# Modulation rows on 32 partitions with fillers between them, angle steps split around the first moving tile, and two weight sums one product later

## The chip, the cores and the metric

The kernel runs on one core of a Trainium2 chip, in one launch. The metric is the time of that launch on the device, in microseconds. The engines are named as in the profile: PE multiplies matrices, PEld is its weight load, DVE (vector), ACT (scalar) and POOL work element by element, SP issues most transfers, and DMA carries them.

## The reference, cut to what matters

The block works on x (2048 rows of 1024) with a conditioning vector c. What concerns us is its head: the modulated norm that makes the input h of the large product, and the angles for the rotary positions.

```
c_act = silu(c)
ada = (c_act @ w_ada + b_ada)[:, None, :]          # 1024 -> 3072
shift, scale, gate = split(ada, 3)
h = rms(x, g_pre) * (1 + scale) + shift            # 2048 x 1024
proj = h @ w_in                                    # 1024 -> 4864
q, k, v, z_a, u_b, v_b, z_b, g_logits = split(proj)
q, k = rope(q, positions), rope(k, positions)      # cos and sin of position * inv_freq
...
y_a = window_attention(q, k, v, sinks) * silu(z_a)
y_b = chunked_gating(gelu(u_b), gelu(v_b)) * silu(z_b)
merged = sigmoid(g_a) * (y_a @ w_proj_a) + sigmoid(g_b) * (y_b @ w_proj_b)
out = x + gate * rms(merged @ w_out, g_post)
```

## The kernel before, in words

**Products.** Every large product is cut into halves three ways and done in the Strassen-Winograd form: seven half-size products (p = 0 to 6) instead of eight. Each uses a weight tile W (a quadrant of the weights, or a sum or difference of quadrants) and a moving tile T (the same of h). Each tile is kept as a rounded high part and a low rest, and `mm3` (L163) multiplies high by high, high by low and low by high: 12 matmuls of 128x512 per product and block. `w_of` (L214) prepares a W: ACT casts the high part at once, and DVE's subtraction for the low part is put on a list that `low_now` (L177) empties later. `want(n)` (L192) prepares all W tiles up to number n; it empties that list first, so the low part of tile n-1 is issued when tile n is prepared. It also calls the transfers some tiles ahead (`fetch_to`, up to a limit `cap`) and the sums that the tile needs (`sum_to`).

**Sums.** `combos` (L243) lists, for one block's seven products, in front of which product each sum of quadrants is issued: s1 and s3 (A21+A22 and A11-A21), s2, s4. For the first four blocks (`first`) DVE makes them, for later blocks POOL. Sums that are kept go to memory a step later.

**Order.** The order on each engine is the order of the program, written out by hand; each engine works through its own list and waits only for data and for free buffers. `step` (L229) runs one product of one block, with hooks before, in the middle and after it; `later(n, f)` hangs f onto the n-th step from now. Tiles have pools with fixed numbers of buffers.

**The head (L761 to L796).** It runs before the first step. Plain filler matmuls (`warm`, L521, a matrix of ones into a bank that is overwritten later) run on PE at the start. The parts, each named as it is used below:

- `positions` and `rope_do(n)` (L663, L621): DVE turns the positions into reduced angles in 24 steps, each a DVE operation on 128x512; `rope_do(n)` issues the next n. `rope_out` (L613) takes their sine on ACT and stores two tiles.
- `squares`, `square_sums`, `rstd`, `rstd_out` (L630 to L661), for half h of the rows of x (`h` = 0, 1): ACT squares eight tiles, DVE adds them, four small PE matmuls sum over partitions, DVE copies (L652), POOL raises to the power -1/2, PE spreads the result over 128 partitions (L658), ACT copies it out (L661).
- `ada_row(hf, kks)` (L680): the modulation rows for half hf of the features. For each of eight slices kk, two matmuls in float32: c_act's column kk, broadcast to 64 columns, against 512 columns of w_ada. Their results stand on partitions 0 to 63 and 64 to 127 of one bank, 64 equal copies of each row. `ada_rows_out` (L690) copies that bank to SBUF on ACT, and `ada_fin` (L694) turns rows into columns by four small matmuls with a picked identity, after which three or four short DVE operations make the scale A and the shift SH (L704, L707).
- `t_part(p, i)` (L751): step i of six for the moving tile of product p: `scaled` (L675, DVE, x times A times the norm), a difference where the product needs one, the high part on ACT (L739, L741), the low part on DVE (L746, L748).

In the order of the program, the head issues 7 angle steps around the squares of the first half, `rstd(0)`, rows 0 and 1, `rstd_out(0)`, 13 angle steps, rows 2 to 7 without a break, W tiles 0 and 1 with both low parts, the loads of the second half of w_ada, the last 4 angle steps, then `ada_rows_out(0)`, `ada_fin(0)`, the squares of the second half between the parts of the first moving tile, W tiles 2 and 3, the sums of the squares, and `rope_out`.

After that the steps begin: product 0 of blocks 0 to 3 (banks X/Y, s and b); behind the third of them `rstd(1)`, behind the fourth `second_half` (L1307): `rstd_out(1)`, all eight slices of `ada_row(1)` on PE, the DVE sums for product 1, and the moving tile of product 1. Then product 1 of the four blocks, and so on to product 6. From block 4 on each block does its seven products in a row.

Of the kernel before, what the change touches and what calls it, by code (L numbers as in the profile page):

```python
# [15 lines left out]
P = 128  # L16
# [34 lines left out]
NFIRST = 4  # L51
# [4 lines left out]
def hybrid_block(ctx: ExitStack, tc: tile.TileContext, xt, x, wada, wgate, wI, wP, wO,  # L56
                 colc, rowc, bs, sinks, ws, pos, consts, mcp, out):
    nc = tc.nc
    act, dve, pool, pe, sp = nc.scalar, nc.vector, nc.gpsimd, nc.tensor, nc.sync
# [3 lines left out]
    sb = ctx.enter_context(tc.tile_pool(name="sb", bufs=1))  # L63
# [23 lines left out]
    def flat(tag, dt=F32):  # L87
        return t2(tag, [P, 512], dt)

    def const(shape, name, dt=F32):  # L90
        return cp.tile(shape, dt, tag=name, name=name)
# [4 lines left out]
    def bank():  # L96
        return pb.tile([P, 512], F32, tag="b", name=nm("b"))
# [35 lines left out]
    ident, mC = cst[:, 0:P], cst[:, P : 2 * P]  # L133
# [19 lines left out]
    def psub(o, a, b, op=ALU.subtract):  # L153
        pool.tensor_tensor(out=o, in0=a, in1=b, op=op)  # L154
# [17 lines left out]
    loads, preps, sums, ready = [], [], [], []  # L172
# [4 lines left out]
    def low_now():  # L177
        while due:
            due.pop(0)()

    def fetch_to(k):
        while cur["load"] < len(loads) and loads[cur["load"]][0] <= min(k, cur["cap"]):
            loads[cur["load"]][1]()
            cur["load"] += 1

    def sum_to(n):
        while cur["sum"] < min(n, len(sums)):
            for f in sums[cur["sum"]]:
                f()
            cur["sum"] += 1  # L190

    def want(n):  # L192

        while cur["prep"] < min(n + 1, len(preps)):
            k = cur["prep"]
            fetch_to(k + 4)
            low_now()
            sum_to(k + 1)
            ready.append(w_of(preps[k]()))
            sum_to(k + 1 + cur["ahead"])  # L200
            fetch_to(k + 5)
            cur["prep"] += 1
# [11 lines left out]
    def w_of(src):  # L214
        w = w_new()
        act.copy(w[:, 0, :], src)  # L216
        due.append(lambda: sub(w[:, 1, :], src, w[:, 0, :].bitcast(F32)))
        return w
# [3 lines left out]
    def later(n, f, post=False):  # L222
        hooks.setdefault((slot[0] + n, post), []).append(f)
# [19 lines left out]
    def combos(env, n, first):  # L243

        def keep(i, t):
            if n is not None:
                later(1, lambda: sp.dma_start(sS[n][i], t))

        second = sub if first else psub


        two = "A22" if first else "A11"

        def s1():
            env["S1"] = flat("S")
            (add if first else lambda o, a, b: psub(o, a, b, ALU.add))(env["S1"], env["A21"], env["A22"])
            keep(0, env["S1"])

        def s3():
            second(env["A21"], env["A11"], env["A21"])  # L260
            keep(2, env["A21"])

        def s2():
            env["S2"] = env[two]
            second(env["S2"], env["S1"], env["A11"])
            keep(1, env["S2"])

        def s4():
            low_now()
            second(env["A12"], env["A12"], env["S2"])  # L270
            keep(3, env["A12"])

        def last():
            return env["A22b"] if first else env["A22"]

        sums.extend([[], [s1], [s2], [], [s3], [s4], []] if first else [[s1, s3], [], [s2], [], [s4], [], []])
        preps.extend([lambda k=k: env[k] for k in ("A11", "S1", "S2", "A12", "A21", "A12")] + [last])

    def stream_fresh(quads, n=None):
# [232 lines left out]
    cact = const([P, 16], "cact")[:, 0:KT]  # L512
# [8 lines left out]
    def warm(n, m=4):  # L521
        for _ in range(n):
            pe.matmul(BK["X"][:, 0 : m * P], ones, wide[:, 0:m, :], start=True, stop=True, skip_group_check=True)
# [89 lines left out]
    def rope_out():  # L613
        for i, k in ((1, 2), (0, 0)):
            t = ropew[:, k, :]
            act.activation(out=t, in_=t, func=AF.Sin)
            sp.dma_start(cs_s[i], t)
# [3 lines left out]
    def rope_do(n):  # L621
        for _ in range(n):
            next(rope_it, None)
# [6 lines left out]
    def squares(h, kts, now=True):  # L630
        for kt in kts:
            if kt == 0:
                sq[h] = flat("e")
                act.activation(out=sq[h], in_=xh[kt][h], func=AF.Square)
            else:
                t = flat("m") if now or kt < 5 else flat("e")
                act.activation(out=t, in_=xh[kt][h], func=AF.Square)
                sq_of.append(t)
                if now:
                    square_sums(h)  # L640

    def square_sums(h):
        while sq_of:
            add(sq[h], sq[h], sq_of.pop(0))
# [11 lines left out]
    def rstd_out(h, b):  # L656
        for i in range(4):
            pe.matmul(b[:, i * P : (i + 1) * P], rs0[h][:, i : i + 1].broadcast_to([P, P]), ident,  # L658
                      start=True, stop=True, skip_group_check=True)
        rbs[h] = flat("e")  # L660
        act.copy(rbs[h], b)  # L661
# [16 lines left out]
    rows = {}  # L678

    def ada_row(hf, kks):  # L680

        if hf not in rows:
            rows[hf] = rows.get("bank") or bank()
        for kk in kks:
            for i in range(2):
                pe.matmul(rows[hf][64 * i : 64 * (i + 1), :], cact[:, kk : kk + 1].broadcast_to([P, 64]),  # L686
                          adaw[hf][kk // 4][:, kk % 4, i * 512 : (i + 1) * 512],
                          start=kk == 0, stop=kk == KT - 1, skip_group_check=True)

    def ada_rows_out(hf):  # L690
        rows[hf, "sb"] = flat("e")
        act.copy(rows[hf, "sb"], rows[hf])

    def ada_fin(hf):  # L694

        o = rows.get("bank") or bank()
        for kt in range(4):
            pe.matmul(o[:, 2 * kt : 2 * kt + 2], rows[hf, "sb"][:, kt * P : (kt + 1) * P], ident[:, 0:P:64],
                      start=True, stop=True, skip_group_check=True)
        o2 = o[:, 0:8].rearrange("p (n two) -> p two n", two=2)  # L700
        c4 = slice(4 * hf, 4 * hf + 4)

        def tt(dst, a, b, op):
            dve.tensor_tensor(out=dst, in0=a, in1=b, op=op)  # L704

        tt(A[:, c4], o2[:, 1], col[:, C_BSC + 4 * hf : C_BSC + 4 * hf + 4], ALU.add)
        dve.scalar_tensor_tensor(out=A[:, c4], in0=A[:, c4], scalar=1.0, in1=col[:, C_GPRE + 4 * hf : C_GPRE + 4 * hf + 4],  # L707
                                 op0=ALU.add, op1=ALU.mult)
        tt(SH[:, c4], o2[:, 0], col[:, C_BSH + 4 * hf : C_BSH + 4 * hf + 4], ALU.add)
        if hf:  # L710
            tt(DS, SH[:, 4:8], SH[:, 0:4], ALU.subtract)
# [39 lines left out]
    def t_part(p, i):  # L751

        if i < 4:
            t_y(p, i)
        if 1 <= i < 5:
            t_d(p, i - 1)
            t_hi(p, i - 1)
        if i >= 2:
            t_lo(p, i - 2)
# [10 lines left out]
    warm(6)  # L770
    rstd(0, BK["Z"])
    ada_row(0, range(0, 2))
    rstd_out(0, BK["W"])
    rope_do(13)
    ada_row(0, range(2, 8))
    want(1)
    low_now()
    ada_load(1)
    cur["cap"] = 3 * NFIRST - 1
    rope_do(26)  # L780
    ada_rows_out(0)
    warm(1, 2)
    ada_fin(0)
    warm(3)
    squares(1, range(0, 2), False)
    for i in range(6):
        t_part(0, i)
        if i == 2:
            want(2)
        elif i == 4:  # L790
            low_now()
        squares(1, range(i + 2, i + 3), False)
    want(NFIRST - 1)
    square_sums(1)
    low_now()
    rope_out()  # L796


# [457 lines left out]
    def run_all():  # L1256
        nonlocal T

        for s in range(NS):
# [38 lines left out]
            if s == 0:  # L1298
# [8 lines left out]
                def second_half():  # L1307
                    rstd_out(1, BK["W"])
                    ada_row(1, range(8))
                    sum_to(2 * NFIRST - 1)  # L1310
                    want(NFIRST)
                    for i in range(6):
                        t_part(1, i)
                        if i == 2:
                            low_now()
                            ada_rows_out(1)
                        elif i == 4:
                            want(NFIRST + 1)

                def second_rows():  # L1320
                    low_now()
                    ada_fin(1)
                    want(NFIRST + 3)
                    for i in range(2):
                        t_part(2, i)
                    low_now()
# [226 lines left out]
```

## Time and profile before

| | |
|---|---|
| median of 3 runs | 1204.56 us (1204.19 to 1206.51) |
| profiled execution, time | 1204.96 us |
| profiled execution, span | 1203.2 us |
| granted PE clock, mean | 0.996 |
| PE busy | 1186.6 us, 99% |
| DVE busy | 867.2 us, 72% |
| ACT busy | 640.4 us, 53% |
| POOL busy | 348.1 us, 29% |
| DMA | 259 GB/s mean |

The span runs from the first to the last instruction, so 1.8 us of the profiled execution's time lie around it. A timeline row has the start, the length of the row (merged from several instructions where x is over 1), engine, line, operation, the tile written and the tiles read, and in brackets how long the engine was idle before it and what it waited for. Names are those of the program without buffer numbers: bankX to bankZ, s and b are PSUM banks, T and W the moving and weight tiles, raw, S, P, x and q buffers. A float32 matmul shows as two passes, so x8 is four matmuls; a matmul of `mm3` shows as one.

### The profile page before, as it was taken

The numbers are of one execution on the slowest core, as the hardware profiler recorded it, in microseconds if no ns is written. First come the engines' busy times: TensorE is split into PE (matmuls) and PEld (weight loads), VectorE is DVE, ScalarE is ACT, GpSimd is POOL, SyncE is SP. The second block draws the span as 40 slices with busy tenths as digits, with TensorE's granted clock in tenths as the row PEclk, the third lists the DMA queues.
The fourth block names the chain that finished last, engine by engine and source line by source line (L and its number), as shares of the span: only waits on it lengthen the run. The fifth ranks groups of instructions, "written<-read, shape, count | busy, mean of one in ns | idle before, by whom it ended". The sixth has DMA issues, their size and how long they took to land.

```text
span 1203.2 us, 17372 instructions
## 1 busy us (share of the span) xinstructions
PE 1186.6 (99%) x5450; PEld 949.4 (79%) x5450; DVE 867.2 (72%) x1319; ACT 640.4 (53%) x1375; POOL 348.1 (29%) x290
## 2 busy tenths in 40 slices
PE   8999999999999999999999999999999999999997
PEld 3677888888877777888888877777778888888886
DVE  7888588668886676355766787565887967767775
ACT  3475454668665676443445766554855412444443
POOL 0001465325266201112211213120033411155443
PEclk9999999999999999999999999999999999999999
DMA  9726997859899998868779997998968988845452
GB/s 351 269 96 210 295 318 259 291 177 294 267 316 345 319 312 276 268 230 272 254 218 282 265 281 247 319 308 256 315 222 289 371 274 266 296 149 186 129 184 88
DMA packets 227972, 311.74 MB, mean 259 GB/s; under 512 B 20900, under 2 KB 102948, under 8 KB 227880
## 3 DMA queue, kind: packets, MB, share of 16 engines
q1 hardware_dynamic: 227408, 309.94, 79.0%
q8 instruction: 43, 0.70, 0.2%
q0 software_dynamic: 176, 0.53, 0.1%
q14 instruction: 49, 0.40, 0.1%
q10 hardware_dynamic: 296, 0.16, 0.1%
HBM read 200.77 MB, written 104.53 MB: 254 GB/s over the span
## 4 chain that ended last, share of the span: by engine, by line
PE 88%; DVE 5%; DMA 2%; ACT 2%; issue 1%; SPq 1%; POOL 0%; DVEq 0%; ACTq 0%; POOLq 0%
PE bankY L168 27%; PE bankX L168 19%; PE bankW L168 12%; PE bankZ L168 12%; PE b L168 5%; PE s L168 4%; PE b L1101 2%; PE b L686 1%; PE s L1051 1%; PE s L1052 1%; PE b L1086 1%; PE b L990 1%; DVE W L151 1%; DVE e L157 1%; DMA e<-za 1%
## 5 line engine op out<-in xcount | busy, mean ns | idle before, releaser
L168 PE MATMUL bankY<-T,W 128*128 128x512 f32 x1578 | 384.6, 392 | 0.3 <-ACT bankY L435 0.2
L168 PEld LDWEIGHTS bankY<-T,W 128*128 128x128 f32 x1578 | 293.2, 188 | 61.9 <-issue 1.0
L151 DVE TENSOR_TENSOR W<-raw,W 128x512 fp32r<-128x512 f32 x327 | 271.9, 838 | 74.4 <-ACT W L216 71.4
L168 PE MATMUL bankX<-T,W 128*128 128x512 f32 x1110 | 271.1, 392 | 1.0 <-DVE T L748 1.0
L216 ACT CAST W<-raw 128x512 fp32r<-128x512 f32 x327 | 201.9, 618 | 129.3 <-PE b L168 39.8
L168 PEld LDWEIGHTS bankX<-T,W 128*128 128x128 f32 x1110 | 206.3, 188 | 44.9 <-DVE T L748 3.0
L168 PE MATMUL bankW<-T,W 128*128 128x512 f32 x684 | 169.4, 395 | 3.8 <-DVE W L151 2.0
L168 PE MATMUL bankZ<-T,W 128*128 128x512 f32 x684 | 166.3, 391 | 0.0
L168 PEld LDWEIGHTS bankW<-T,W 128*128 128x128 f32 x684 | 127.9, 189 | 32.2 <-DVE T L151 3.1
L168 PEld LDWEIGHTS bankZ<-T,W 128*128 128x128 f32 x684 | 127.4, 188 | 27.7 <-ACT T L387 1.6
L154 POOL TENSOR_TENSOR S<-x,x 128x512 f32<-128x512 f32 x28 | 37.7, 1356 | 238.7 <-DMA x<-yb 110.3
L154 POOL TENSOR_TENSOR raw<-raw,raw 128x512 f32<-128x512 f32 x46 | 74.9, 1628 | 91.3 <-issue 44.8
L154 POOL TENSOR_TENSOR S<-raw,raw 128x512 f32<-128x512 f32 x23 | 35.2, 1529 | 172.5 <-DMA x<-e 63.9
L157 DVE TENSOR_TENSOR e<-bankY,e 128x512 f32<-128x512 f32 x43 | 29.7, 691 | 59.8 <-PE bankY L168 52.7
L151 DVE TENSOR_TENSOR T<-x,T 128x512 fp32r<-128x512 f32 (+1 forms) x105 | 69.7, 711 | 3.5 <-ACT T L387 3.1
L168 PE MATMUL b<-T,W 128*128 128x512 f32 x282 | 69.3, 390 | 0.0
L168 PEld LDWEIGHTS b<-T,W 128*128 128x128 f32 x282 | 52.9, 188 | 11.0
L168 PE MATMUL s<-T,W 128*128 128x512 f32 x246 | 60.0, 389 | 0.0
L387 ACT CAST T<-x 128x512 fp32r<-128x512 f32 x100 | 56.0, 618 | 2.7 <-PE s L168 2.1
L168 PEld LDWEIGHTS s<-T,W 128*128 128x128 f32 x246 | 46.2, 188 | 9.6
L154 POOL TENSOR_TENSOR raw<-S,raw 128x512 f32<-128x512 f32 x23 | 33.1, 1437 | 69.4 <-DVE W L151 53.2
L1080 ACT ACTIVATE P<-P,rc 128x128 f32<-128x128 f32 x128 | 44.5, 396 | 12.3 <-DVE rc L1076 12.2
(271 smaller groups left out, 1439.1 us busy)
## 6 DMA issues: line engine op xcount, KB each, us to landing
raw<-in_wI SPq DMA_DIRECT2D x127, 256.0 KB, 4.6
raw<-sS SPq DMA_DIRECT2D x92, 256.0 KB, 5.1
g<-e SPq DMA_DIRECT2D x64, 256.0 KB, 4.0
sS<-raw SPq DMA_DIRECT2D x43, 256.0 KB, 4.3
T<-in_wada SPq DMA_DIRECT2D x16, 512.0 KB, 7.9
q<-q SPq DMA_DIRECT2D x64, 128.0 KB, 5.4
q<-k_s SPq DMA_DIRECT2D x64, 128.0 KB, 4.9
raw<-m SPq DMA_DIRECT2D x32, 256.0 KB, 4.1
```

The lines of the kernel that those rows point to most:

```text
L151: dve.tensor_tensor(out=o, in0=a, in1=b, op=ALU.subtract)
L154: pool.tensor_tensor(out=o, in0=a, in1=b, op=op)
L157: dve.tensor_tensor(out=o, in0=a, in1=b, op=ALU.add)
L168: pe.matmul(o, w[:, i, sl], t[:, j, kt, :], start=start and kt == kts[0] and n == 0, stop=stop and kt == last and n == 2, skip_group_check ...
L216: act.copy(w[:, 0, :], src)
L387: act.copy(T[p][:, 0, kt, :], rs[kt])
L686: pe.matmul(rows[hf][64 * i : 64 * (i + 1), :], cact[:, kk : kk + 1].broadcast_to([P, 64]), adaw[hf][kk // 4][:, kk % 4, i * 512 : (i + 1) ...
L990: pe.matmul(b[:, ch * P : (ch + 1) * P], st["v", h][:, ch, :], wT[:, c, :], start=True, stop=True)
L1051: pe.matmul(o, q[:, g, :], k[:, 0, :], start=True, stop=False)
L1052: pe.matmul(o, q[:, g, :], k[:, 1, :], start=False, stop=True)
L1080: act.activation(out=st["P", kv][:, g, 0:P], in_=st["P", kv][:, g, 0:P], func=AF.Copy, scale=st["rc", kv][:, g : g + 1])
L1101: pe.matmul(o[own, :], v[:, k, own], st["pv", kv][k], start=k == 1, stop=k == 0)
```

## The change

- In `combos`, block 4 alone (the first whose sums POOL makes) gets s1 and s3 in front of product 1 instead of product 0.
- `ada_row` broadcasts c_act to 32 columns instead of 64, so that the two rows stand on partitions 0 to 31 and 32 to 63; the copy and the small matmuls behind it use these 64 partitions.
- Between the slices 2 to 7 of the first half stand five fillers of 256 columns, `warm(1, 2)`. The second half has none.
- 9 angle steps instead of 13 follow `rstd_out(0)`; the other 8 of the 24 are issued behind the second half's square sums and the low part of W tile 3, ahead of `rope_out`.
- W tile 1 is prepared at part 2 of the first moving tile and W tile 2 at part 4, instead of before the tile and at part 2; each low part comes with the next.

```
-        sums.extend([[], [s1], [s2], [], [s3], [s4], []] if first else [[s1, s3], [], [s2], [], [s4], [], []])
+        sums.extend([[], [s1], [s2], [], [s3], [s4], []] if first else
+                    [[], [s1, s3], [s2], [], [s4], [], []] if n == NFIRST else [[s1, s3], [], [s2], [], [s4], [], []])
...
-                pe.matmul(rows[hf][64 * i : 64 * (i + 1), :], cact[:, kk : kk + 1].broadcast_to([P, 64]),
+                pe.matmul(rows[hf][32 * i : 32 * (i + 1), :], cact[:, kk : kk + 1].broadcast_to([P, 32]),
...
-        act.copy(rows[hf, "sb"], rows[hf])
+        act.copy(rows[hf, "sb"][0:64], rows[hf][0:64, :])
...
-            pe.matmul(o[:, 2 * kt : 2 * kt + 2], rows[hf, "sb"][:, kt * P : (kt + 1) * P], ident[:, 0:P:64],
+            pe.matmul(o[:, 2 * kt : 2 * kt + 2], rows[hf, "sb"][0:64, kt * P : (kt + 1) * P], ident[0:64, 0:64:32],
...
     rstd_out(0, BK["W"])
-    rope_do(13)
-    ada_row(0, range(2, 8))
-    want(1)
+    rope_do(9)
+    for kk in range(2, 8):
+        ada_row(0, (kk,))
+        if kk < 7:
+            warm(1, 2)
+    want(0)
     low_now()
     ada_load(1)
     cur["cap"] = 3 * NFIRST - 1
-    rope_do(26)
     ada_rows_out(0)
...
     for i in range(6):
         t_part(0, i)
-        if i == 2:
-            want(2)
-        elif i == 4:
-            low_now()
+        if i in (2, 4):
+            want(i // 2)
         squares(1, range(i + 2, i + 3), False)
     want(NFIRST - 1)
     square_sums(1)
     low_now()
+    rope_do(26)
     rope_out()
```

## The prediction

> **Bounds now.** I read the page first, then the timeline of the first 70 us engine by engine (the head is where nearly all of the diff lies), then the table of windows for the clock, then the place where block 4's sums run.
>
> ```profile
> PE 1186.6 (99%) x5450; PEld 949.4 (79%) x5450; DVE 867.2 (72%) x1319; ACT 640.4 (53%) x1375; POOL 348.1 (29%) x290
> ...
> PE 88%; DVE 5%; DMA 2%; ACT 2%; issue 1%; SPq 1%; POOL 0%; DVEq 0%; ACTq 0%; POOLq 0%
> ```
>
> PE is the bound: busy 99% of the span, and 88% of the chain that ended last. Behind the head PE never has much to wait for, so a microsecond that the head loses stays lost, and one that it wins is won. So the question is what the edits do to PE's own list in the head, and to the DVE work that PE waits for there.
>
> The timeline of PE in the head, rows with L686 being the modulation rows, L523 fillers, L649 and L658 the two halves of the norm, L168 the products:
>
> ```profile
> 15.60 3.53 PE L686 MATMUL b<-T,cact 128*64 128x512 f32 x8
> ...
> 20.21 5.37 PE L686 MATMUL b<-T,cact 128*64 128x512 f32 x24
> 25.51 0.70 PE L523 MATMUL bankX<-ones 128*128 128x256 f32 x2
> ...
> 27.18 2.82 PE L523 MATMUL bankX<-ones 128*128 128x512 f32 x6
> ...
> 40.19 0.95 PE L649 MATMUL bankZ<-ones,e 128*128 128x2 f32 x8
> 41.00 3.03 PE L168 MATMUL b<-T,W 128*128 128x512 f32 x12
> 43.86 1.05 PE L658 MATMUL bankW<-cst,rs 128*128 128x128 f32 x8
> 44.85 7.09 PE L686 MATMUL b<-T,cact 128*64 128x512 f32 x32
> ...
> 63.83 0.61 PE L168 MATMUL bankW<-T,W 128*128 128x512 f32 x2
> 66.45 4.14 PE L168 MATMUL bankW<-T,W 128*128 128x512 f32 x10 [2.00 <-DVE W L151]
> ```
>
> From 15.60 to 27.18 PE goes from row to row with no wait in brackets: it sets the pace there. From 40.19 to 51.9 it is again back to back. At 66.45, the start of product 2, it has waited 2.00 us for DVE's low part of a weight tile. DVE in the same stretch (L558 to L609 angle steps, L151 low parts, L704 the modulation columns, L652 the copy inside the norm, L675 the moving tile):
>
> ```profile
> 21.42 0.43 DVE L558 TENSOR_SCALAR T<-T 128x512 f32<-128x512 f32 x1
> ...
> 23.82 1.28 DVE L151 TENSOR_TENSOR W<-raw,W 128x512 fp32r<-128x512 f32 x2
> 25.03 0.42 DVE L560 TENSOR_SCALAR T<-T 128x512 f32<-128x512 f32 x1
> ...
> 26.67 0.43 DVE L560 TENSOR_SCALAR T<-T 128x512 f32<-128x512 f32 x1
> 27.35 0.16 DVE L704 TENSOR_TENSOR AS<-b,col 128x4 f32<-128x4 f32 x1 [0.26 <-PE b L698]
> ...
> 39.11 0.69 DVE L151 TENSOR_TENSOR W<-raw,W 128x512 fp32r<-128x512 f32 x1
> 41.18 0.16 DVE L652 COPY ss<-bankZ 128x4 f32<-128x4 f32 x1 [1.38 <-PE bankZ L649]
> ...
> 46.12 1.41 DVE L675 SCALAR_TENSOR_TENSOR q<-q,AS,e 128x512 f32<-128x512 f32 x2
> ...
> 65.71 1.29 DVE L151 TENSOR_TENSOR W<-P,W 128x512 fp32r<-128x512 f32 x2
> ```
>
> Two stretches of the window table (columns: length, then busy time of PE, PEld, DVE, ACT, POOL, then clock, DMA share, GB/s) say where DVE has room and where it has none:
>
> ```profile
> 39.80:44.91 5.11, 5.11 (x33) 4.38 (x33) 2.15 (x4) 0.00 (x0) 1.69 (x2) 1.00 1.04 387
> 46.12:66.40 20.28, 18.32 (x86) 11.92 (x82) 19.52 (x36) 11.35 (x20) 0.00 (x0) 1.00 0.24 86
> ```
>
> Ahead of 44.91 DVE is idle for 3.0 of 5.1 us, in waits for PE and others; from 46.12 to 66.40 it is busy 19.5 of 20.3 us. So the second moving tile's start at 46.12 fixes, by DVE's list alone, when product 2 can begin.
>
> **Fillers: 3.5 us.** Two filler passes of 256 columns took 0.70 us (25.51). [...] Five fillers stand in PE's list between rows that already run back to back: 5 x 0.70 = 3.5 us; by the bare size 5 x 0.47 = 2.35, and with a tenth for the way back into the rows (an estimate from the same 0.23) 4.0. [...]
>
> What hides the fillers? Nothing: behind the last row stand, one after the other, ACT's copy, four small matmuls and DVE's row 27.35, which had waited 0.26 us for PE. The edit also takes 4 angle steps and one low part off DVE ahead of 27.35, but DVE was ready 0.26 us before PE, so that is worth nothing, and after it DVE only waits longer. All that follows moves by s = 3.5 us; times below are given without s.
>
> **Narrow rows: nothing.** No 32-wide row is in this trace. The nearest rows are the 64-wide and the 128-wide passes of 512 columns (minimum, median, maximum in ns):
>
> ```profile
> L523 PE MATMUL bankX<-ones x24: 379/593/1222, 1.1 to 29.4; 128*128 128x512 f32 x22, 128*128 128x256 f32 x2
> ```
> ```profile
> L686 PE MATMUL b<-T,cact x64: 592/592/1061, 15.6 to 51.3; 128*64 128x512 f32 x64
> ```
>
> A pass takes 592 or 593 ns at either width. That 24 narrow passes fit in 5.37 us (0.22 each, against 0.47) is because the two rows of a slice, on different columns of the array, run side by side. With 32 columns there are still two rows per slice, so I take the same 5.37 and 7.09 us. The bounds are the first two rivals. The copy of 64 partitions instead of 128 and the small matmuls over 64 keep their lengths along the free axis; I take them as they are.
>
> **W tiles: hidden.** One low part (1.28 for two, at 23.82) moves from before the first moving tile to between it and the square sums. DVE ran without gaps there, so the low part of W tile 3 ends at 39.80 + 0.64 = 40.44, and PE wants it at 41.00; the square sums end at 39.75 instead of 39.11, and PE wants them at 40.19. Both still in time, by some 0.5 us. If that cover were gone, it would cost what is over.
>
> **Angle steps: 2.55 us.** In the old places the eight took 23.82 - 21.42 = 2.40 and 27.10 - 25.03 = 2.07, together 4.47 us. Now they run from 40.44 to 44.91. Queued behind them on DVE is the copy of the norm sums (41.18 before), and behind that copy, on other engines, these:
>
> ```profile
> 41.71 1.50 POOL L148 TENSOR_TENSOR rs<-pw,nhalf 128x4 f32<-128x4 f32 x1
> ```
> ```profile
> 45.01 0.58 ACT L661 COPY e<-bankW 128x512 f32<-128x512 f32 x1 [7.81 <-PE bankW L658]
> ```
>
> POOL ended at 43.21, 2.03 us after the copy's start, and PE used the result at 43.86. Now POOL ends at 44.91 + 2.03 = 46.94 and PE, done with product 0 at 43.86, stands idle for 3.1 us. ACT's copy of the spread norm ended at 45.59, 1.73 us behind 43.86; now at 48.67, and DVE can begin the second moving tile at 48.67 instead of 46.12: 2.55 us later. DVE itself would be there a little sooner: 44.91 + 2.15 of work from the window + 1.21 up to 46.12 = 48.27. The idle 3.0 us before 44.91 thus take up part of the 4.47. From there DVE's full list carries the 2.55 to 66.40: product 2 starts at 69.0. PE, 3.1 us late at 63.83, comes to it at 66.93, does its two matmuls and waits 1.5 us, so DVE still decides.
>
> The sines on ACT and their two stores on SP move behind the angles too. ACT has nothing until the copy at 48.1, SP's list behind the stores holds constants and sums that are made later still: nothing.
>
> **Clock: nothing.** The windows are cut at the steps of the granted clock:
>
> ```profile
> 12.29:15.70 3.41, 1.08 (x10) 1.07 (x12) 3.13 (x7) 0.00 (x0) 0.00 (x0) 1.00 1.03 412
> 15.70:19.12 3.42, 3.42 (x9) 0.65 (x9) 3.32 (x8) 0.00 (x0) 1.56 (x2) 0.51 1.03 416
> ...
> 63.50:66.91 3.41, 1.41 (x7) 0.86 (x6) 2.83 (x5) 3.04 (x6) 0.00 (x0) 1.00 0.00 0
> 66.91:70.32 3.41, 3.41 (x10) 2.69 (x9) 2.69 (x6) 2.30 (x4) 0.00 (x0) 0.51 0.23 77
> ```
>
> Twice a stretch with PE busy for 1.1 or 1.4 of 3.4 us is followed by 3.4 us at half clock. The second time ten matmuls took 4.14 us instead of 10/12 of 3.03, 1.6 us lost. The new idle 3.1 us at 43.86 should do the same to the second half's rows; the wait of 1.5 us at product 2 may not. If the gate shuts at the rows, they end 1.7 us later, DVE waits about as much for the second half's modulation columns, and product 2 then runs at full clock: +1.6 and -1.6. If it shuts at product 2 as before, nothing changes. Either or both: plus or minus 1.7. [...]
>
> **Sums: nothing.** The place where block 4's sums run:
>
> ```profile
> 107.06 1.37 POOL L154 TENSOR_TENSOR S<-raw,raw 128x512 f32<-128x512 f32 x1 [63.85 <-DMA x<-e]
> 107.20 1.79 DVE L151 TENSOR_TENSOR T<-x,T 128x512 fp32r<-128x512 f32 x1
> ...
> 111.24 1.07 PE L168 MATMUL bankW<-T,W 128*128 128x512 f32 x4
> ...
> 112.30 0.68 DVE L151 TENSOR_TENSOR T<-x,T 128x512 fp32r<-128x512 f32 x1
> ...
> 116.61 2.91 PE L168 MATMUL bankZ<-T,W 128*128 128x512 f32 x12
> ```
>
> s1 is the POOL row, s3 and a rotary product follow it. While they run, a DVE subtraction takes 1.79 instead of 0.68 us, and PE's twelve matmuls from 111.24 take 5.37 instead of 2.9: 2.5 us are lost there. But POOL waits for loads only, so a later place in the program lets the rotary product go first and s1 and s3 right behind it, in the same stretch. I take 0, with -2.5 as the other end.
>
> **The sum.** 3.5 + 2.55 = 6.05 us on the profiled execution's 1204.96: 1211.0. That execution lies 0.4 above the median of the runs shown, so I forecast 1204.56 + 6.05 = 1210.6. Its own range is 2.35 + 2.55 - 1.7 = +3.2 to 4.0 + 2.55 + 1.7 = +8.25: 1207.8 to 1212.8. About 0.2%, or 2.4 us, is what can be told from no change.
>
> **Rivals.**
> - *The gate counts columns in use.* Two 32-wide rows fill half the columns that two 64-wide ones do, and in the second half no filler stands between them. Then the window after 19.1 stays at half clock (+1.7 on s) and the 7.09 us of rows become 10.5 to 14.2, PE instead of DVE decides product 2, and the total is +8 to +11: 1212.6 to 1215.6. For it: all that the trace shows of the gate is that 64-wide rows open it (15.70 to 19.12, then full clock). Against it: full clock from then on although every other part of the head uses the array unevenly. 0.13.
> - *Not slower: a row's time goes with its width.* If a 32-wide pass took half of a 64-wide one, rows 0 and 1 would lose up to 1.77 of 3.53 us and rows 2 to 7 2.68 of 5.37, and s = 3.5 - 4.45 = -0.95. The second half's rows gain nothing while DVE decides, so 2.55 - 0.95 = +1.6: 1206.2, no change to be told. It decides from a step of 0.22 us per slice and pass instead of the 0.45 of 5.37/12. For it: passes of half the width did come at half the distance, 0.22 against 0.47. Against it: 592 ns each at both widths. 0.15.
> - *The gate stays open.* If neither 3.1 nor 1.5 us of idleness shuts it, product 2 loses its 1.6 us no more: 6.05 - 1.6 = +4.45, 1209.0. Against it: the window from 63.50. 0.10.
> - *The sums do get out of the way.* If s1 and s3 start only after the moving tile of product 6, 2.5 us come back: +3.55, 1208.1. Against it: POOL's wait for data alone. 0.14.
>
> **How the numbers follow.** The forecast has 0.48. The range from 1205.5 to 1216.5 leaves out the lower half of the second rival, and what would lie beyond the first: together about 0.15. Faster by over 0.2% needs the second and third rivals and a full clock at once (1.6 - 2.5 - 1.6): 0.05. Within 0.2% falls most of the second and a little of the third: 0.13. Slower: 0.82.
>
> **What would show it.** Right: 32-wide passes of 592 ns in pairs, each filler adding about 0.7 us between them; row 27.35 near 30.9; the angle steps directly ahead of the L652 copy; PE idle for some 3 us in front of L658 at product 1; the second moving tile 6 us later than 46.12, product 2 near 72.5; the three POOL rows still together beside slow DVE rows. Wrong: a step of 0.22 us between rows, a clock of 0.5 over the second half's rows for more than one window, or PE's twelve matmuls of product 6 without waits.

## The result and the profile after

| | before | changed |
|---|---|---|
| median | 1204.42 us (1204.19 to 1206.51, 4 runs) | 1212.65 us (1211.25 to 1214.55, 4 runs) |
| ratio, 95% interval | | 1.0066 (1.0045 to 1.0086) |
| profiled execution, span | 1203.2 us | 1209.5 us |
| its granted clock | 0.996 | 0.998 |

The changed kernel is slower by 0.66%, 8 us by the ratio. The forecast was 1210.6 us, +6.05, in a range from 1205.5 to 1216.5. The profiled execution of the changed kernel, 1211.25 us, is the fastest of its four, and its span has grown by 6.3 us; the other three, at granted clocks of 0.996, 0.994 and 0.994, lie up to 3.3 us higher. Such differences between executions of one kernel are taken up at the end. Lines of the changed kernel have numbers 1 to 3 higher: L687 are the rows, L524 the fillers, L659 the spread of the norm, L653 its copy.

PE's timeline answers to the rows shown of before:

```profile
16.20 1.91 PE L687 MATMUL b<-T,cact 128*32 128x512 f32 x8
18.36 1.16 PE L659 MATMUL bankW<-cst,rs 128*128 128x128 f32 x8 [0.25 <-POOL rs L148]
19.45 1.05 PE L687 MATMUL b<-T,cact 128*32 128x512 f32 x4
20.43 0.70 PE L524 MATMUL bankX<-ones 128*128 128x256 f32 x2
21.06 1.05 PE L687 MATMUL b<-T,cact 128*32 128x512 f32 x4
22.04 0.70 PE L524 MATMUL bankX<-ones 128*128 128x256 f32 x2
...
44.14 2.99 PE L168 MATMUL b<-T,W 128*128 128x512 f32 x12
50.48 2.06 PE L659 MATMUL bankW<-cst,rs 128*128 128x128 f32 x8 [3.35 <-POOL rs L148]
52.46 7.78 PE L687 MATMUL b<-T,cact 128*32 128x512 f32 x32
60.17 1.66 PE L168 MATMUL bankW<-T,W 128*128 128x512 f32 x6
...
72.40 0.61 PE L168 MATMUL bankW<-T,W 128*128 128x512 f32 x2
74.75 2.57 PE L168 MATMUL bankW<-T,W 128*128 128x512 f32 x10 [1.74 <-DVE W L151]
77.16 2.88 PE L168 MATMUL bankZ<-T,W 128*128 128x512 f32 x12
```

Three things are to be seen. A slice with its filler has a period of 22.04 - 20.43 = 1.61 us, where slices alone came every 0.86 (12 matmuls in pairs, 5.37 us for six slices). The spread at 50.48 waits 3.35 us for POOL, where the kernel before had no wait. And it takes 2.06 us instead of 1.05: half clock. The window table, cut at the steps of the granted clock, has the reason (PE's busy time first, the clock third from the end):

```profile
47.13:50.53 3.40, 0.05 (x1) 0.05 (x1) 3.37 (x7) 1.15 (x2) 1.90 (x2) 1.00 0.36 132
50.53:53.95 3.42, 3.42 (x12) 2.08 (x14) 1.53 (x4) 1.10 (x2) 0.00 (x0) 0.50 0.81 287
53.95:57.36 3.41, 3.41 (x18) 0.91 (x16) 3.41 (x7) 1.24 (x2) 0.00 (x0) 1.00 0.37 139
```

PE's wait fills one window, and the next is granted half. Below, the gate is said to shut where the granted clock falls to half, and to open where it is full again. DVE in the same place: the last low part, the first and the last of the eight angle steps, the copy, the second moving tile.

```profile
43.09 0.69 DVE L151 TENSOR_TENSOR W<-raw,W 128x512 fp32r<-128x512 f32 x1
43.69 0.42 DVE L559 TENSOR_SCALAR T<-T 128x512 f32<-128x512 f32 x1
...
47.85 0.43 DVE L561 TENSOR_SCALAR T<-T 128x512 f32<-128x512 f32 x1
48.19 0.16 DVE L653 COPY ss<-bankZ 128x4 f32<-128x4 f32 x1
...
53.24 1.42 DVE L676 SCALAR_TENSOR_TENSOR q<-q,AS,e 128x512 f32<-128x512 f32 x2 [1.89 <-ACT e L662]
```

Side by side, the starts in the two profiled executions; the last column is what has been lost up to there:

| event on PE, or as named | before | changed | later by |
|---|---|---|---|
| first norm | 14.62 | 15.22 | 0.60 |
| row 2 | 20.21 | 19.45 | -0.76 |
| modulation columns (DVE) | 27.35 | 30.32 | 2.97 |
| second norm | 40.19 | 43.23 | 3.04 |
| its spread | 43.86 | 50.48 | 6.62 |
| product 1 | 51.86 | 60.17 | 8.31 |
| product 2, ten matmuls | 66.45 | 74.75 | 8.30 |
| product 2, block 1 | 70.42 | 77.16 | 6.74 |
| block 4 | 124.80 | 130.94 | 6.14 |
| end of the span | 1203.2 | 1209.5 | 6.3 |

From row 2 to the columns the fillers cost 3.73 us; from the second norm to product 1 the late angle steps cost 5.27; at product 2 the kernel before lost time to a half-clock window that the changed one did not have in this execution. Behind block 4 nothing more is lost or won: the head decides.

### The profile page after: what moved, and what is told of

Its sections match the earlier page's. It is cut to its first block, busy times and chain, and to the rows that moved or that the text cites. A ratio compares the mean times of both kernels' runs of the same rounds, so it can differ in the third digit from the quotient of the medians.

```text
span 1209.5 us, 17394 instructions
## 1 busy us (share of the span) xinstructions
PE 1192.7 (99%) x5460; PEld 950.1 (79%) x5460; DVE 862.1 (71%) x1319; ACT 641.2 (53%) x1375; POOL 352.6 (29%) x290
## 4 chain that ended last, share of the span: by engine, by line
PE 90%; DMA 3%; DVE 3%; ACT 1%; issue 1%; POOL 0%; SPq 0%; DVEq 0%; ACTq 0%; POOLq 0%
PE bankY L168 29%; PE bankX L168 20%; PE bankW L168 12%; PE bankZ L168 12%; PE b L168 4%; PE s L168 4%; PE b L1103 2%; DMA T<-in_wada 2%; PE s L1053 1%; PE s L1054 1%; PE b L992 1%; PE b L1088 1%; DMA q<-in_xt 1%; PE b L687 1%; DVE W L151 1%
## 5 line engine op out<-in xcount | busy, mean ns | idle before, releaser
L151 DVE TENSOR_TENSOR W<-raw,W 128x512 fp32r<-128x512 f32 x327 | 266.0, 819 | 73.3 <-ACT W L216 70.7
L154 POOL TENSOR_TENSOR x<-x,m 128x512 f32<-128x512 f32 x20 | 29.2, 1468 | 77.3 <-DMA x<-e 67.6
```

What stands on the lines that cost most here:

```text
L151: dve.tensor_tensor(out=o, in0=a, in1=b, op=ALU.subtract)
```

## The experiments

Each run is compared with runs of the kernel before on the same chip; the ratio is that of the two, with its 95% interval, and 0.1% is 1.2 us.

**The fillers taken out of the changed kernel.**

```
     for kk in range(2, 8):
         ada_row(0, (kk,))
-        if kk < 7:
-            warm(1, 2)
```

> The changed kernel without its five fillers; all else as changed. Theory (each filler costs the 0.75 us that it shows in the changed trace, nothing hides it, and narrow rows keep the gate open by themselves): rows 2 to 7 take about 5.4 us instead of 9.1, the whole is 3.75 us below the changed kernel, 1208 to 1209.5. Rival (the gate counts columns in use, the fillers are needed): the clock falls to 0.5 over the first half's rows too, and the time is that of the changed kernel or more, 1212 and up.

Measured: 1208.70 us, ratio 1.0035 (1.0024 to 1.0047). Rows 2 to 7 take 5.34 us without any filler, against 5.37 in the kernel before, where the granted clock over them was 0.99 to 1.00:

```profile
15.59 3.51 PE L687 MATMUL b<-T,cact 128*32 128x512 f32 x8
19.03 1.21 PE L659 MATMUL bankW<-cst,rs 128*128 128x128 f32 x8
20.17 5.34 PE L687 MATMUL b<-T,cact 128*32 128x512 f32 x24
```

The fillers are 0.31% of the changed kernel's 0.66%, and the narrow rows did not need them.

**The angle steps of the changed kernel put back.**

```
-    rope_do(9)
+    rope_do(13)
...
+    rope_do(26)
     ada_rows_out(0)
...
     low_now()
-    rope_do(26)
     rope_out()
```

> The changed kernel with the 24 angle steps in their old places; all else as changed. Theory (the late steps hold up the copy of the norm sums on DVE, and cost 2.5 to 4 us): PE does not wait ahead of the spread of the second norm, the second moving tile starts some 3.5 to 4 us later than before instead of 7.1, and the whole is at 1208.5 to 1210. Rival (DVE's idle time takes the steps up, the fillers are the whole loss): 1212, as the changed kernel.

Measured: 1207.28 us, 1.0018 (1.0009 to 1.0028), less than was expected. PE has no wait at the spread, and the spread and the rows behind it take 1.05 and 7.06 us, where the kernel before took 1.05 and 7.09 at a granted clock of 1.00:

```profile
47.04 1.05 PE L659 MATMUL bankW<-cst,rs 128*128 128x128 f32 x8
48.02 7.06 PE L687 MATMUL b<-T,cact 128*32 128x512 f32 x32
```

So the late steps are 0.48% of the 0.66%, nearly 6 us, or 3.0 to 8.5 us by the two intervals; the forecast's 2.55 is less than half of it. The rest of the change, with the fillers in it, costs only 0.18% or 2.2 us here, less than the 0.31% that came back when the fillers were taken out, though within the intervals.

**The narrow rows alone, on the kernel before.** The edits are those of the diff's `ada_row`, `ada_rows_out` and `ada_fin`.

> The kernel before with the rows on 32 columns and the copy and small matmuls that go with them, no other edit. Theory (width costs and saves nothing): 1204.5, within 1 us of the kernel before, passes of 592 ns, full clock over the second half's rows. Rival on the gate: half clock over the rows, 1208 and up. Rival on the width: rows in half the time, the first moving tile 4 us earlier, 1201 to 1203.

Measured: 1203.98 us, 0.9997 (0.9986 to 1.0009). In its trace the second half's rows take 7.06 us, against 7.09 before, where the granted clock was 1.00. The first line is from there; the second, from the source view of the rows of the changed kernel, has the pass (minimum, median, maximum in ns):

```profile
45.09 7.06 PE L686 MATMUL b<-T,cact 128*32 128x512 f32 x32
```
```profile
L687 PE MATMUL b<-T,cact x64: 592/592/1063, 16.2 to 59.6; 128*32 128x512 f32 x64
```

The median is that of the 64-wide passes. Both rivals on the width fall: rows of half the width are neither quicker nor do they shut the gate.

**The angle steps alone, on the kernel before.**

```
-    rope_do(13)
+    rope_do(9)
...
-    rope_do(26)
     ada_rows_out(0)
...
     low_now()
+    rope_do(26)
     rope_out()
```

> The kernel before with 9 angle steps instead of 13 behind the first norm and the other 8 ahead of the sines, no other edit. Theory: PE waits about 3 us ahead of the spread of the second norm, a half-clock window falls on the second half's rows or on product 2, and the whole is 2.5 to 4 us above the kernel before, 1207 to 1208.5. Rival (the idle time of DVE takes the steps up): 1204.5, no wait of PE at that place.

Measured: 1210.71 us, 1.0049 (1.0032 to 1.0066), more than was expected: the steps alone cost 6 us, 3.9 to 8.0 by the interval. The wait is there, and behind it two windows of half clock (45.6 to 52.4), so that the rows, still 64 wide, take 9.00 instead of 7.09 us:

```profile
46.49 2.08 PE L658 MATMUL bankW<-cst,rs 128*128 128x128 f32 x8 [2.92 <-POOL rs L148]
48.50 9.00 PE L686 MATMUL b<-T,cact 128*64 128x512 f32 x32
57.42 1.66 PE L168 MATMUL bankW<-T,W 128*128 128x512 f32 x6
```

**The same, with PE kept busy in the wait.**

```
+                    for _ in range(3):
+                        pe.matmul(BK["W"], ones, wide, start=True, stop=True, skip_group_check=True)
                     rstd_out(1, BK["W"])
                     ada_row(1, range(8))
```

> The kernel before with the eight angle steps late, as in the run with the steps alone, and three fillers of 512 columns on PE ahead of the spread of the second norm, in the time in which PE would wait. Theory (a good part of the steps' cost is the clock: the wait shuts the gate over the rows): rows of 7.1 us instead of 9.0, product 2 some 2 us sooner, 1208 to 1209 where the steps alone had 1210.7. Rival (the clock nets to nothing, as the prediction had it): 1210.7, as the steps alone.

Measured: 1207.58 us, 1.0023 (1.0012 to 1.0034). The fillers bring 0.26%, some 3 us, though nothing uses what they compute; what is left of the steps, 0.23% or 2.8 us (1.4 to 4.1), is about the 2.55 that the prediction had for the wait itself.

```profile
45.04 2.74 PE L1309 MATMUL bankW<-ones 128*128 128x512 f32 x6
48.09 1.16 PE L658 MATMUL bankW<-cst,rs 128*128 128x128 f32 x8 [0.31 <-POOL rs L148]
49.17 7.09 PE L686 MATMUL b<-T,cact 128*64 128x512 f32 x32
56.19 1.65 PE L168 MATMUL bankW<-T,W 128*128 128x512 f32 x6
```

The spread comes as late as with the steps alone, 19.6 us behind the modulation columns in both (28.53 to 48.09 here, 26.91 to 46.49 there), but the rows take 7.09 us, as in the kernel before at a granted clock of 1.00: spread and rows, which took 11.1 us with the steps alone, take 8.2. The intervals of the two totals just touch (1.0032 to 1.0066 and 1.0012 to 1.0034), so it is the traces, the same wait with and without half clock behind it, that decide between "a wait" and "a wait and what it does to the clock".

**The eight steps behind the norm's copy instead of ahead of it.**

```
     low_now()
-    rope_do(26)
-    rope_out()
...
-                later(NFIRST - 2, lambda: rstd(1, BK["Z"]), True)
+                later(NFIRST - 2, lambda: (rstd(1, BK["Z"]), rope_do(26), rope_out()), True)
```

> The changed kernel with the eight late angle steps issued directly behind the copy of the norm sums instead of ahead of it; the same work on DVE. Theory (what the late steps cost is PE's wait, the half clock over the rows that follows from it, and ACT's casts of the moving tile that queue behind the copy of those rows): no wait ahead of the spread, rows of 7.1 us at full clock, product 2 only about 3 us late by DVE's list, the whole about 2 us below the changed kernel, 1210 to 1211. Rival (DVE's amount of work decides, wherever the eight stand): as the changed kernel, 1212.5.

Measured: 1210.21 us, 1.0043 (1.0029 to 1.0057); its interval overlaps that of the changed kernel, 1.0045 to 1.0086, so the total alone does not tell the two theories apart. The trace does: PE does not wait ahead of the spread, the rows take 7.06 us, and DVE starts the second moving tile 53.22 - 45.63 = 7.6 us behind the copy, with the eight steps in that time. PE now waits for the moving tile in product 1, 0.40 and 1.14 us, and product 2's block 1 comes 75.94 - 31.63 = 44.3 us behind the modulation columns, against 77.16 - 30.32 = 46.8 in the changed kernel. The same DVE work, placed one instruction later, is 2.5 us cheaper there in these two traces. The clock seems not free of cost here either: behind the two waits in product 1 six matmuls take 2.81 us where they took 1.66 in the changed kernel, and the next twelve 3.38 instead of 2.88. The 1.65 us are about the 1.6 that one half-clock window cost at product 2 of the kernel before; that it was one window is an estimate from these lengths.

```profile
48.28 1.05 PE L659 MATMUL bankW<-cst,rs 128*128 128x128 f32 x8
49.26 7.06 PE L687 MATMUL b<-T,cact 128*32 128x512 f32 x32
...
61.26 2.81 PE L168 MATMUL bankW<-T,W 128*128 128x512 f32 x6
63.87 3.38 PE L168 MATMUL bankZ<-T,W 128*128 128x512 f32 x12
```

**The fillers alone, on the kernel before,** its rows still 64 wide.

> The kernel before with the five fillers between the slices 2 to 7 of the first half's rows, which stay 64 wide; no other edit. Theory (0.75 us for each filler on the path, nothing hides it): the first moving tile 3.75 us later, 1208.3. Rival (the waits later in the head take a part up): 1206 to 1207.

Measured: 1209.09 us, 1.0037 (1.0025 to 1.0049): 4.5 us, somewhat more than the 3.75 of the five alone, which its interval, 3.0 to 5.9 us, contains. The period of a slice with its filler is 1.64 us (20.76 to 22.40 in its trace), 0.78 more than a slice. Nothing behind is seen to take any of it up.

**The W tiles alone, on the kernel before.**

> The kernel before with W tiles 1 and 2 prepared at parts 2 and 4 of the first moving tile and their low parts one later, no other edit. Theory (one low part of 0.6 us more on DVE ahead of the square sums, which PE has 0.5 us to spare for): the low part of W tile 3 about 0.6 us later, the norm at 40.2 and the spread at 43.9 not later than by 0.3 us, the whole within 0.5 us of the kernel before, 1204.5. Rival (this edit gains what the run without fillers has over the run with the steps alone): 1202.5.

Measured: 1205.02 us, 0.9998 (0.9988 to 1.0008). The low part that was moved costs nothing, as the prediction had it.

**The two sums alone, on the kernel before.**

> The kernel before with block 4's two sums one product later, no other edit. Theory (POOL takes them right behind the rotary product, in nearly the same stretch): about 0.6 us below the kernel before at product 6, as in the changed kernel, 1204.0, not to be told in the total; DVE rows of 1.8 us are still there beside POOL. Rival (they get out of the way): PE does product 6 of block 0 in 2.9 us instead of 5.4, 1202.

Measured: 1204.63 us, 0.9996 (0.9987 to 1.0005). POOL's three rows are still together, in the other order, and slow DVE rows are still beside them; the same part of the changed kernel's timeline:

```profile
114.60 1.77 POOL L154 TENSOR_TENSOR x<-x,m 128x512 f32<-128x512 f32 x1 [64.17 <-DMA x<-e]
...
115.13 1.79 DVE L151 TENSOR_TENSOR x<-x,wT 128x512 f32<-128x512 f32 x1
116.33 1.74 POOL L154 TENSOR_TENSOR S<-raw,raw 128x512 f32<-128x512 f32 x1
116.84 1.78 DVE L151 TENSOR_TENSOR T<-x,T 128x512 fp32r<-128x512 f32 x1
...
118.15 1.63 POOL L154 TENSOR_TENSOR raw<-raw,raw 128x512 f32<-128x512 f32 x1
118.54 0.68 DVE L157 TENSOR_TENSOR e<-s,e 128x512 f32<-128x512 f32 x1
119.14 1.18 DVE L151 TENSOR_TENSOR x<-x,Tt 128x512 f32<-128x512 f32 x1
```

**The sums really delayed.** If POOL waits only for loads, the loads are the handle. The kernel before, with the diff's edit of `sums` and the two quadrants loaded three products later:

```
+        late = 4 if n == NFIRST else 1
-        plan = [(0, "A11", "raw"), (1, "A21", "raw"), (1, "A22", ("P", "P", "x", "x")[n] if first else "raw"),
+        plan = [(0, "A11", "raw"), (late, "A21", "raw"), (late, "A22", ("P", "P", "x", "x")[n] if first else "raw"),
...
-        for off, key, tag in plan:
+        for off, key, tag in sorted(plan, key=lambda z: z[0]):
```

> The kernel before with block 4's two sums one product later, and with the two quadrants that they read loaded three products later, so that POOL has to wait. Theory (POOL's rows slow DVE down while DVE makes the last moving tile of the head): only the rotary product, one POOL row, is left beside it, PE does product 6 of block 0 in about 4 us instead of 5.4, and the whole is 1 to 2 us below the kernel before, 1203. Rival (DVE would be as late without POOL): no change at product 6, 1204.6. If the later load holds up ACT's cast of the sum, blocks 4 and 5 would show PE waiting for W.

Measured: 1202.09 us, 0.9973 (0.9963 to 0.9982), faster than the kernel before. Only the rotary product is left beside the moving tile, the sums run when DVE's part of it is done, and product 6 of block 0 has lost its waits: 3.17 us for twelve matmuls where before went from 111.24 to 116.61. Beside the sums DVE rows are slow still, 1.78, 1.77 and 1.78 us from 117.20 on, but PE waits for none of those, and in blocks 4 and 5 it does not wait for W.

```profile
106.92 1.30 POOL L154 TENSOR_TENSOR x<-x,m 128x512 f32<-128x512 f32 x1 [62.81 <-ACT T L741]
116.82 1.61 POOL L154 TENSOR_TENSOR S<-raw,raw 128x512 f32<-128x512 f32 x1 [8.60 <-DVE W L151]
```
```profile
111.80 3.17 PE L168 MATMUL bankW<-T,W 128*128 128x512 f32 x12
114.82 2.93 PE L168 MATMUL bankZ<-T,W 128*128 128x512 f32 x12
```

**And PE kept busy in the wait at product 2.** On top of the late loads, two fillers with weights of zero, added onto the bank that product 2 of block 0 writes next, so that they change nothing in it:

```
+                def fill():
+                    for _ in range(2):
+                        pe.matmul(BK["W"], zero[:, 0:1].broadcast_to([P, P]), wide, start=False, stop=True, skip_group_check=True)
+                later(2 * NFIRST, fill)
```

> The kernel with the late loads (the kernel before, block 4's two sums one product later and their quadrants loaded three products later), and two fillers of 512 columns with weights of zero, added onto block 0's own bank, ahead of product 2, where PE waits 2.0 us for DVE. Theory (that wait shuts the gate in some executions, at 1.6 us each, and DVE sets product 2's start whether PE idles or not): the ten matmuls of product 2 take 2.6 us in every execution, the whole is 0.5 to 1.6 us below the late loads alone, 1200.5 to 1201.5. Rival (the gate is shut by less, or the fillers run past the wait): 1202 or more.

Measured: 1199.86 us, 0.9957 (0.9944 to 0.9971), better than was expected and the fastest of all. Its five runs lie within 0.64 us (1199.48 to 1200.12), where the kernel before spread over 3.7 us in the same session (1203.59 to 1207.3).

```profile
64.06 1.88 PE L1340 MATMUL bankW<-ones,zero 128*128 128x512 f32 x4
65.38 1.03 PE L170 MATMUL bankW<-T,W 128*128 128x512 f32 x2
66.67 2.56 PE L170 MATMUL bankW<-T,W 128*128 128x512 f32 x10 [0.27 <-DVE W L153]
```

The wait of 2.00 us is down to 0.27, and ten matmuls take 2.56 us, against 3.55 in the trace of the late loads alone and 4.14 in that of the kernel before. DVE's low parts come 38.3 us behind the modulation columns, as in the late loads alone, so the gain at this place is put down to the clock. In the totals the two intervals overlap (0.9944 to 0.9971 and 0.9963 to 0.9982): the 0.16% on top of the late loads is not secured by them, though all five runs lie below the lowest with the late loads alone, 1200.54 us in another session.

## Why the prediction was right, and where it was wrong

*Direction and range.* Right: slower, 1212.65 inside 1205.5 to 1216.5, and 8.2 us where 6.05 were forecast. The interval, 5.4 to 10.4 us, contains the forecast, so the total alone does not show that a term was wrong; the single runs do.

*Fillers, 3.5 us.* Right in mechanism and nearly in size: 3.73 us by the trace (period 1.61 against 0.86, five times 0.75), 0.31% by taking them out, 0.37% alone. The bare size is 0.47 us (six passes of 512 columns in 2.82 us at 27.18, so two of 256 in 0.47), and 0.70 is 0.23 more. No run shows that these 0.23 us are a price for leaving the rows or for going back into them, on which the range's upper 4.0 rests. What the changed kernel's trace shows in its place: 0.63 us pass from a filler's start to the next slice's (20.43 to 21.06), and the slice itself takes 0.98 instead of 0.86 (21.06 to 22.04). The length of the row, 0.70, holds the tail of the last pass, which the next matmuls overlap (20.43 + 0.70 = 21.13, and they start at 21.06), and so it was in part luck that five of them came so near.

*Narrow rows, nothing.* Right, by the run with them alone and by 592 ns. That the pair's half distance does not come from the width was the right reading; that the two rows run side by side is in the trace of before, where two passes of rows are under way together from 20.20 on and the next two start together at 20.68.

*W tiles, hidden.* Right.

*Angle steps, 2.55 us.* The wait itself was found: PE idle 3.1 us forecast, 3.35 measured, and 2.8 us of cost when the clock is kept up. What failed is the next step, **"Clock: nothing"**. The prediction let the half-clock window move from product 2 to the second half's rows and netted +1.6 and -1.6. In the profiled execution of the changed kernel this is just what happened, one window at the spread and none at product 2, and its span is up by 6.3 us; but that is the fastest of the four. The runs with the steps alone, with and without fillers in the wait, put the clock at 3 us on top of the wait. Two things were missed. One is the price: in the run with the steps alone the gate stayed shut for two windows, not one, and product 2 was slow as well, ten matmuls in 3.94 us, where the kernel before took 4.14 in its half-clock window and the changed kernel 2.57. The other is the path. The spread itself, which the moving tile waits for, ran at half clock, 2.06 us instead of 1.05. And the prediction let slow rows reach DVE by the modulation columns only; they reached it earlier. On ACT the casts of the moving tile's second half stand behind `ada_rows_out`, and this copy waits for the last row on PE:

```profile
60.35 0.58 ACT L693 COPY e<-b 64x512 f32<-64x512 f32 x1 [3.17 <-PE b L687]
60.83 0.62 ACT L740 CAST T<-wT 128x512 fp32r<-128x512 f32 x1
```
```profile
61.48 0.69 DVE L151 TENSOR_TENSOR T<-wT,T 128x512 fp32r<-128x512 f32 x1 [1.28 <-ACT T L740]
```

The wait of 1.28 us in DVE's full list is new, and it is how slow rows reach product 2 in spite of DVE's being the bound there. In the kernel before the same copy had come at 52.03 and DVE's list was barely touched.

*Sums, nothing.* Nearly right, for the reason given. Product 6 of block 0 did win 0.6 us in the changed kernel's trace (117.96 to 122.76 is 4.80 us, against 5.37), since the burst now falls so that only two and a half DVE rows are slow (1.79, 1.78 and 1.18 us); the total shows no difference from none.

*Rivals.* The gate that counts columns, and time by width: refuted by the narrow rows alone. The open gate: refuted at the spread, behind which the granted clock was 0.50. The sums that get out of the way: not in this change, but the price of 2.5 us was about right. With the late loads product 6 of block 0 takes 114.82 - 111.80 = 3.02 us instead of 5.37, and the whole gains 0.27%, 3.3 us (2.2 to 4.5).

What stays open: fillers, steps, narrow rows, W tiles and sums alone add up to 0.37 + 0.49 - 0.03 - 0.02 - 0.04 = 0.77%, against 0.66 (0.45 to 0.86) together. The intervals allow both that they add and that half-clock windows shared between them are counted twice. One such sharing can be seen in the traces, but is not shown in the totals: with narrow rows PE comes to product 2 a little later and waits 1.7 us there instead of 2.0, and the ten matmuls behind this wait took 2.57 us in the changed kernel and 2.60 with the steps put back. Behind 2.0 us they took 4.14 in the kernel before, 3.94 with the steps alone and 3.55 with the late loads, though 2.56 in the run with fillers in the wait at the spread. That would make the fillers cheaper in the changed kernel, where the rest beside the steps cost 0.18%, than alone, 0.37%.

## What to carry to other kernels

Ahead of an instruction on which PE waits through a chain of engines (copy, power, spread), nothing belongs on the first engine's list that can stand behind it: here one instruction's place was worth 2.5 us at product 2 for the same work. A wait of PE for two or three microseconds can have a second price in the clock behind it, here 1.6 us at product 2 and about 3 behind the spread, so price it with the rows that follow, and fill it with matmuls that change nothing; but fillers between matmuls that already ran back to back were a plain loss here, 0.31 to 0.37% for five. The sums' later place in the program did not delay POOL, which waited for data only (ratio 0.9996); moving their data did (0.9973).

## What the runs showed of the hardware

**Half-clock stretches came in windows of 3.4 us, at a phase that differed from run to run.** In the kernel before the two stretches that the prediction shows last 3.42 and 3.41 us and begin 66.91 - 15.70 = 51.2 us apart, fifteen times 3.41; the one of the changed kernel, from 50.53, lasts 3.42 us, and that of the run with the steps alone, from 45.60, twice 3.40. Counted from 15.70 in steps of 3.41 us, 50.53 lies 0.7 us behind a step and 45.60 lies 2.6. In the kernel before the wait of 2.00 us at product 2 lay within one window, 63.50 to 66.91, and the gate shut; in the changed kernel the wait of 1.74 us there, from 73.01 to 74.75, was cut by a window's edge at 74.42, seven windows behind 50.53, and the gate did not shut (ten matmuls in 2.57 us). Length alone does not tell the two cases apart: in the trace with fillers in the wait at the spread the wait at product 2 was 2.00 us again, from 68.77 to 70.77, and the ten matmuls took 2.56 us. Executions of that run lay between 1204.87 us, at a granted clock of 0.999, and 1210.01, at 0.994. So the phase may explain part of the 3 to 5 us between executions of one kernel; this is an estimate. The last run's five executions, with the waits in product 6 taken away by the late loads and the one at product 2 by the fillers, all had 0.998 and lay within 0.64 us; this fits, but rests on five runs.

No one share of busy time sorts these windows. In the changed kernel PE was busy for 0.05 of 3.40 us before the gate shut, in the kernel before for 1.08 and 1.41 of 3.41. In the run with the steps alone it was 1.37 of 3.40, and the gate stayed shut behind a window with 2.51:

```profile
42.20:45.60 3.40, 1.37 (x6) 0.77 (x5) 3.29 (x8) 1.15 (x2) 1.06 (x2) 0.99 0.43 159
45.60:49.00 3.40, 2.51 (x10) 2.08 (x12) 1.76 (x3) 0.34 (x1) 0.84 (x1) 0.50 0.82 284
49.00:52.40 3.40, 3.40 (x10) 0.95 (x8) 3.12 (x5) 1.38 (x3) 0.00 (x0) 0.50 0.65 249
```

In the changed kernel it stayed open behind less, 2.00 of 3.41 us from 71.01 and 1.91 of 3.41 from 118.80. In product 1 of the run with the steps behind the copy the slow matmuls come behind a wait of 1.14 us; if the window before them held this wait alone, 3.41 - 1.14 = 2.27 us of it were busy, an estimate.

**Beside POOL, DVE rows that read two SBUF tiles were slow.** In the changed kernel, beside POOL's three rows, subtractions of two SBUF tiles took 1.79 and 1.78 us instead of 0.69, but the row at 118.54, which reads PSUM and one SBUF tile, took its usual 0.68 beside POOL's row at 118.15. What in the chip makes the difference is not shown here.
